# Hybrid decoder trunk on one core: longest query blocks first, and the wait for attention moved into the out-projection

## The chip, the cores and the metric

One core of a Trainium2 chip runs the whole layer in one launch. The metric is device time in microseconds (us) of one execution, lower is better. TensorE (PE) does the matmuls and the transposes, PEld is its weight load, DVE, ACT and POOL do elementwise work, and the queue of SyncE (SP) issues nearly all DMAs.

## The reference, cut to what matters

```python
h = rmsnorm(x, norm_mix_w) * (1 + sc1) + sh1            # 2048 tokens x 1024
hq, hf, hi, hg, sq, sk, sv, iq, ik, iw, cu = split(h @ w_in)
o_a = hgrn2_mixer(hq, hf, hi, hg)                       # linear recurrence, 512 columns
# o_b, 256 columns, one block of 128 queries at a time (16 blocks, j = 0..15):
score = einsum('bqh,bqhs->bqs', iw, relu(q_idx . k_idx)) # 8 indexer heads, keys <= query
sel   = top_k(score, 256)                               # per query
o_b   = softmax(q . k[sel]) @ v[sel]                    # 4 heads of 64
o_c = conv_module(cu)                                   # 256 columns
x = x + g1 * (concat[o_a, o_b, o_c] @ w_out)            # the out-projection
h = rmsnorm(x, norm_mlp_w) * (1 + sc2) + sh2
x = x + g2 * (relu(h @ mlp_w1)**2 @ mlp_w2)             # d_ff 4096
out = rmsnorm(x, final_norm_w)
```

Block j sees (j + 1) x 128 keys, so its indexer, its top-k search and its attention all grow with j.

## The kernel before

**Order of the whole.** Tokens go in four blocks of 512 (b = 0 to 3). First `in_block` projects all four and writes the queries, the keys, the values and the mixers' outputs to DRAM. Then, for each b, comes the out-projection `out_block(b)` and the MLP: `mlp_block` for b = 0 to 2 and `strassen_block` for the last. Matrix products run in three passes of split fp32 (high x high, low x high, high x low); `split` makes the halves, the high one with a copy on ACT (L256), the low one with a subtraction on POOL (L264).

**Background work.** The query blocks j = 0 to 5 are handled during `in_block`, those from `J1` = 6 on beside the MLPs of b = 0, 1 and 2. Each block j is three generators: `index_gen` (scores: PE L752, ACT L754, DVE L759), `topk_gen` (a threshold search on DVE, 8 passes of L861, ending with the bias at L832) and `attn_gen` (PE L909, L931, L943 and L955, DVE L911, ACT L939 and L940, POOL L941), which the search of j appends to its queue when it is done. They sit in the queues "idx", "tk" and "at". A main loop that reaches a `yield` calls `step`, which gives each queue a credit of `rates[q]`; a generator runs until its own yields have used the credit up. Credits are the program's own nominal nanoseconds. The yields are, with n the keys of the block: indexer 8.8 n in all; search 1000 + 7 (1.05 n + 1300) + 2000 + 3.6 n, and 0.6 n after it has handed over (11.55 n + 12100 in all); attention 1.1 n + 4 (1.1 n + 300 c + 300), with c its chunks of 512 keys. A generator that is blocked yields `None` and loses the credit at hand. At most two blocks have their scores alive, and at most two their bias. The tile scheduler then places the instructions on each engine and may let a later one go first where an earlier one isn't ready in its own timeline.

**One MLP block in steps.** `mlp_order` gives 32 `m1` units (first product, L357, PSUM "mm") and 32 `m2` units (second product through `n_unit`, L1169, PSUM "ax", two buffers, evicted by DVE L1313). With group g = 6 it yields "prep" before `m2` of g = 6, and with g = 7 "out" before `m1`. So a block has 52 steps up to "prep", 4 to "out", and 8 after it; `out_block` itself makes 4.

**Where attention is waited for.** "prep" calls `prep_out(b + 1)`, which calls `drain_bg(4 (b + 1) + 3)`: all background queues are pumped with 3000 each, again and again, until the last query block of that token block is done. Then `mix_tiles(b + 1, 0)` loads rows 0 to 3 of the mixed activations (the recurrence). "out" calls `out_block`, which loads x, then `mix_tiles(b, 1)`, rows 4 to 7: rows 4 and 5 are attention, 6 and 7 the convolution. For each of four column blocks q of 256 it runs the first half of the rows (kh = 0) and the second (kh = 1), two token pairs each, in two PSUM buffers "ax" (for b = 0 in "at" and "mm" by turns), 24 matmuls for a pair; DVE L1212 multiplies by the gate, POOL L1216 adds to x.

**Sums for the last MLP.** The queue "ts" runs during `mlp_block(2)`: `tsum_gen` loads 24 units of weight quarters into "tsr", makes four sums each on DVE (L1411, L1412, L1414, L1415) and stores them to `ts_d`. A unit yields 2.0 and the rate is 1.0. At "out" what is left is drained.

Of the kernel before, what the change touches and what calls it, by code (L numbers as in the profile page):

```python
# [8 lines left out]
F32 = mybir.dt.float32  # L9
# [7 lines left out]
OP = mybir.AluOpType  # L17
# [3 lines left out]
P = 128  # L21
# [17 lines left out]
FAST = 979  # L39
# [6 lines left out]
PTB, PM, LB, LB2 = 1, 1, 4, 4  # L46
PREP = 14
R1 = [1126, 1216, 1594]
R2 = [950, 1650, 900]
AXB = 2  # L50
NX = 20
STG = 3
# [25 lines left out]
def trunk(ctx, tc, x, c, ada_w, ada_b, norm_mix_w, norm_mlp_w, w_in, hg_lb_logits,  # L78
# [22 lines left out]
    def nm(s):  # L101
        uid[0] += 1
        return f"{s}_{uid[0]}"

    def dma(o, i):
        return nc.sync.dma_start(o, i)
# [7 lines left out]
    def ps_ax():  # L114
        return px["p"].tile([P, 512], F32, tag="ax", bufs=px["ax"], name=nm("ax"))
# [880 lines left out]

    adone = set()

    def drain_bg(upto=None):
        while any(queues[q] for q in ("idx", "tk", "at")):  # L1000
            if upto is not None and upto in adone:
                break
            for q in ("at", "tk", "idx"):
                pump(q, 3000.0)

    rates = {"fast": FAST, "conv": CR, "ada": 800.0, "ts": 1.0, "idx": R1[0], "tk": R1[1], "at": R1[2]}

    def step():
        for q in ("fast", "conv", "ada", "idx", "tk", "at", "ts"):
# [96 lines left out]

    def out_specs():
        return [([(0, 256, wout[kh * 512:(kh + 1) * 512, q * 256:(q + 1) * 256])], "wo", 4, 256)
                for q in range(4) for kh in range(2)]

    def mlp1_specs(g):
        return [([(0, P, w1[:, (g * 4 + f) * P:(g * 4 + f + 1) * P])], "w1") for f in range(4)]
# [8 lines left out]
    def add_topk(k, js):  # L1121
        for j in js:
            queues["idx"].append(index_gen(k, j))
            queues["tk"].append(topk_gen(k, j))
# [33 lines left out]
            elif what == "m2":  # L1158
                specs += mlp2_specs(g)

    def n_part(ps, tpair, act, w, first, last):
        hh, hl = act
        hi, lo = w
        for t in range(2):
            tok = tpair * 2 + t
            n = 0
            for aa, ww in ((hh, hi), (hl, hi), (hh, lo)):
                for f in range(4):
                    T.matmul(ps[:, t * 256:(t + 1) * 256], aa[f][:, tok * P:(tok + 1) * P],  # L1169
                             ww[:, f, :], start=(first and n == 0 and (last or t == 0)),  # L1170
                             stop=(last and n == 11), skip_group_check=not (first and last))
                    n += 1

    def n_unit(act, consume):
        w = next_w()
        for tpair in range(2):
            ps = ps_ax()
            n_part(ps, tpair, act, w, True, True)
            consume(tpair, ps.rearrange("p (t m) -> p t m", t=2))

    def mix_tiles(b, kh):
        hh, hl = [], []
        for k in range(4):
            hi = mp.tile([P, TB], F32R, tag="hh", bufs=HB, name=nm("mh"))
            lo = mp.tile([P, TB], F32R, tag="hl", bufs=HB, name=nm("ml"))
            r = mp.tile([P, TB], F32, tag="hr", bufs=MR, name=nm("mr"))
            dma(r, mx_d[b][kh * 4 + k])
            split(r, hi, lo)
            hh.append(hi)
            hl.append(lo)  # L1190
        return hh, hl

    def out_block(b, mix0):
        xts = []
        for t in range(4):
            xt = xp.tile([P, D], F32, tag="xt", bufs=4, name=nm("x1"))
            dma(xt, x2d[b * TB + t * P:b * TB + (t + 1) * P, :])
            xts.append(xt)
        mixes = [mix0, mix_tiles(b, 1)]
        for q in range(4):  # L1200
            gq = mp.tile([P, 256], F32, tag="gq", bufs=GQ, name=nm("gq"))
            dma(gq, g_d[2][:, q * 256:(q + 1) * 256].to_broadcast([P, 256]))
            pss = []
            for kh in range(2):
                w = next_w()
                for tp_ in range(2):
                    if kh == 0:
                        pss.append(ps_ax() if b else (ps_at, ps_mm)[q % 2]())
                    n_part(pss[tp_], tp_, mixes[kh], w, kh == 0, kh == 1)
                    if kh == 1:  # L1210
                        tmp = mp.tile([P, 2, 256], F32, tag="hr", bufs=MR, name=nm("ot"))
                        V.tensor_tensor(tmp, pss[tp_].rearrange("p (t m) -> p t m", t=2),  # L1212
                                        gq[:, None, :].to_broadcast([P, 2, 256]), OP.mult)
                        for t in range(2):
                            dst = xts[tp_ * 2 + t][:, q * 256:(q + 1) * 256]
                            G.tensor_tensor(dst, dst, tmp[:, t, :], OP.add)  # L1216
            yield
        for t in range(4):
            xt = xts[t]
            dma(x1_d[b][t], xt)  # L1220
            dump = xp.tile([P, D], BF16, tag="tf", bufs=2, name=nm("xdump"))
            rs = rstd_of(xt, D, dump, "x1")
            V.tensor_scalar(xt, xt, rs, None, op0=OP.mult)
        x1s[b] = xts
# [4 lines left out]
    def mlp_last(acc, act, b):  # L1229
        fw = xp.tile([P, D], F32, tag="xt", bufs=4, name=nm("fw"))  # L1230
        dma(fw, final_norm_w[None, :].to_broadcast([P, D]))
        ss = mp.tile([P, 4, 4], F32, tag="ssq", bufs=1, name="ssq")
        s1 = mp.tile([P, 4], F32, tag="ss1", bufs=1, name="ss1")
        for q in range(4):
            sl = slice(q * 256, (q + 1) * 256)
            gq = mp.tile([P, 256], F32, tag="gq", bufs=GQ, name=nm("gq"))
            dma(gq, g_d[5][:, sl].to_broadcast([P, 256]))
            xq_ = xp.tile([P, 4, 256], F32, tag="xt", bufs=4, name=nm("xq"))
            for t in range(4):
                dma(xq_[:, t], x1_d[b][t][:, sl])  # L1240
            if q == 3:
                V.tensor_tensor(acc[:, :, sl], acc[:, :, sl], gq[:, None, :].to_broadcast([P, 4, 256]), OP.mult)
                V.tensor_tensor(acc[:, :, sl], acc[:, :, sl], xq_, OP.add)

            def consume(tp_, src, q=q, sl=sl, gq=gq, xq_=xq_):
                tt = range(tp_ * 2, tp_ * 2 + 2)
                dst = acc[:, tp_ * 2:tp_ * 2 + 2, sl]
                gv = gq[:, None, :].to_broadcast([P, 2, 256])
                if q == 3:
                    tmp = mp.tile([P, 2, 256], F32, tag="hr", bufs=MR, name=nm("lt"))  # L1250
                    V.tensor_tensor(tmp, src, gv, OP.mult)
                    V.tensor_tensor(dst, dst, tmp, OP.add)
                else:
                    V.tensor_tensor(dst, dst, src, OP.add)  # L1254
                    V.tensor_tensor(dst, dst, gv, OP.mult)
                    V.tensor_tensor(dst, dst, xq_[:, tp_ * 2:tp_ * 2 + 2], OP.add)
                for t in tt:
                    dump = mp.tile([P, 256], BF16, tag="ld", bufs=2, name=nm("ld"))
                    A.activation(dump, acc[:, t, sl], AF.Square, accum_out=ss[:, t, q:q + 1])
                if q == 3:  # L1260
                    rs = s1[:, tp_ * 2:tp_ * 2 + 2]
                    V.tensor_reduce(rs, ss[:, tp_ * 2:tp_ * 2 + 2, :], axis=AX.X, op=OP.add)
                    rpow(rs, rs, 2, 1.0 / D)
                    for t in tt:
                        V.scalar_tensor_tensor(acc[:, t, :], acc[:, t, :], s1[:, t:t + 1], fw,
                                               op0=OP.mult, op1=OP.mult)
                        dma(out2d[b * TB + t * P:b * TB + (t + 1) * P, :], acc[:, t, :])

            n_unit(act, consume)
            if (b, q) == (NB - 2, EQ):  # L1270
                st3["early"]()
            yield

    def mlp_block(b):
# [3 lines left out]
        for what, g, f in mlp_order(b):  # L1278
# [23 lines left out]
            elif g == 7 and b == NB - 2:  # L1302
                yield from mlp_last(acc, hid.pop(g), b)
                return
            else:
                hg_ = hid.pop(g)
                for q in range(4):
                    def consume(tp_, src, q=q):
                        dst = acc[:, tp_ * 2:tp_ * 2 + 2, q * 256:(q + 1) * 256]
                        if g == 0:  # L1310
                            A.copy(dst, src)
                        else:
                            V.tensor_tensor(dst, dst, src, OP.add)  # L1313

                    n_unit(hg_, consume)
                    yield
        fw = xp.tile([P, D], F32, tag="xt", bufs=4, name=nm("fw"))
        dma(fw, final_norm_w[None, :].to_broadcast([P, D]))
# [320 lines left out]
    mixes = {}  # L1639

    def prep_out(b):
        if 4 * b + 3 >= J1:
            drain_bg(4 * b + 3)
        mixes[b] = mix_tiles(b, 0)

    def run_out(b):
# [49 lines left out]
    S3 = ExitStack()  # L1696
    tp2 = S3.enter_context(tc.tile_pool(name="tk2", bufs=1, reuse_waits="tile"))
    k2 = TK(tp2, 2048, SB)
    add_topk(k2, range(J1, 16))
    rates.update({"idx": R2[0], "tk": R2[1], "at": R2[2]})  # L1700
    for b in range(NB):
        if b == NB - 2:
# [33 lines left out]
```

## Time and profile before

| | us |
|---|---|
| median of 3 runs | 3050.99 (3048.38 to 3053.09) |
| profiled execution, its time | 3049.01 |
| its span, first to last instruction | 3047.3 |
| PE busy in the span | 2831.7 |

The span and the profiled execution's own time differ by 1.7 us, which lies around the instructions. The granted clock of PE over the whole span is 0.968 of full speed. A busy PE isn't the same as a PE at full clock: the windows list the granted clock beside the busy time.

### The profile page before, as it was taken

What the parts mean: (1) busy time and instruction counts of PE and PEld (TensorE: products, weight loads), DVE (VectorE), ACT (ScalarE), POOL (GpSimd) and SP (SyncE); (2) the same over time, 40 slices, a digit from 0 to 9 for tenths busy, and PEclk for the clock granted to TensorE, in tenths of its full rate; (3) what the DMA queues carried; (4) which work ended last, traced back from release to release, by engine and by line L of the source; (5) the groups of instructions that cost most, each with busy time, mean ns of one, the idle gap of its engine ahead of it and who ended that gap; (6) DMA issues with size and microseconds to landing.
All of it is one profiled execution on the core that took longest, in us unless ns stands there. A gap on an engine that the chain in (4) does not pass through costs nothing. (4 is left out here: it accounts for less than half of the span.)

```text
span 3047.3 us, 50794 instructions
## 1 busy us (share of the span) xinstructions
PE 2831.7 (93%) x18352; PEld 2549.2 (84%) x18352; DVE 2007.2 (66%) x3673; ACT 1541.7 (51%) x2885; POOL 1796.5 (59%) x1530
## 2 busy tenths in 40 slices
PE   6989989899999999999999999999899997989997
PEld 4878868777887889899988898898788896879997
DVE  7796486977536343757766756577888631487787
ACT  3436354535413234555556555646464543456654
POOL 7565152234305265666777666778676664767775
PEclk9989989999999989999999999999999997999999
DMA  8866756665655343444455444555999943465533
GB/s 269 279 195 237 228 183 222 198 204 179 224 181 165 120 157 100 122 133 138 151 171 193 144 142 136 156 159 177 284 316 298 310 146 107 135 201 180 179 124 114
DMA packets 479416, 560.10 MB, mean 184 GB/s; under 512 B 32615, under 2 KB 371884, under 8 KB 479148
## 3 DMA queue, kind: packets, MB, share of 16 engines
q1 hardware_dynamic: 478992, 556.65, 58.2%
q8 instruction: 145, 2.38, 0.3%
q14 instruction: 123, 1.01, 0.1%
q10 hardware_dynamic: 156, 0.07, 0.0%
HBM read 458.30 MB, written 98.31 MB: 183 GB/s over the span
## 5 line engine op out<-in xcount | busy, mean ns | idle before, releaser
L264 POOL TENSOR_TENSOR wlo<-wraw,whi 128x512 fp32r<-128x512 f32 x514 | 719.5, 1421 | 417.3 <-ACT whi L256 275.0
L256 ACT CAST whi<-wraw 128x1024 fp32r<-128x1024 f32 x257 | 269.7, 1049 | 391.1 <-PE ax L1169 154.5
L759 DVE SCALAR_TENSOR_TENSOR s<-r,iw_s,s 128x512 f32<-128x512 f32 (+3 forms) x266 | 267.8, 1007 | 160.6 <-ACT r L754 159.1
L357 PE MATMUL mm<-ah,wk 128*128 128x512 f32 x1104 | 297.2, 404 | 11.0 <-DVE q L586 3.1
L1169 PE MATMUL ax<-whi,hh 128*128 128x256 f32 x1600 | 276.2, 288 | 22.3 <-DVE acc L1254 8.2
L1169 PE MATMUL ax<-whi,hl 128*128 128x256 f32 x1600 | 274.7, 285 | 2.4 <-POOL hl L264 2.4
L1169 PE MATMUL ax<-wlo,hh 128*128 128x256 f32 x1600 | 272.0, 285 | 0.0
L357 PE MATMUL mm<-ah,whi 128*128 128x512 f32 x936 | 259.2, 403 | 13.6 <-DVE slo L470 3.2
L941 POOL TENSOR_TENSOR pT<-L,pT 128x512 fp32r<-128x512 f32 (+3 forms) x160 | 198.6, 1243 | 116.2 <-ACT pT L940 96.2
L357 PE MATMUL mm<-al,whi 128*128 128x512 f32 x936 | 258.9, 399 | 0.0
L1169 PEld LDWEIGHTS ax<-whi,hh 128*128 128x128 f32 x1600 | 231.4, 191 | 32.7 <-DVE acc L1313 14.6
L357 PEld LDWEIGHTS mm<-ah,wk 128*128 128x128 f32 x1104 | 207.7, 193 | 55.8 <-ACT k L577 3.5
L357 PE MATMUL mm<-ah,wlo 128*128 128x512 f32 x936 | 252.4, 394 | 0.0
L1169 PEld LDWEIGHTS ax<-whi,hl 128*128 128x128 f32 x1600 | 230.5, 191 | 6.2 <-POOL hl L264 3.7
L528 POOL TENSOR_TENSOR cside<-cside,ctap 128x512 f32<-128x512 f32 x112 | 159.1, 1421 | 122.1 <-ACT ctap L527 107.1
L1169 PEld LDWEIGHTS ax<-wlo,hh 128*128 128x128 f32 x1600 | 227.7, 190 | 1.5
L357 PEld LDWEIGHTS mm<-ah,whi 128*128 128x128 f32 x936 | 175.9, 192 | 52.0 <-DVE slo L470 4.0
L754 ACT ACTIVATE r<-ix 128x512 f32<-128x512 f32 (+3 forms) x256 | 141.4, 552 | 145.3 <-PE ix L752 139.0
L357 PEld LDWEIGHTS mm<-al,whi 128*128 128x128 f32 x936 | 176.3, 191 | 35.8
L357 PEld LDWEIGHTS mm<-ah,wlo 128*128 128x128 f32 x936 | 175.2, 189 | 35.8
L861 DVE TENSOR_SCALAR_CACHE_REDUCE cum<-s,ssm 128x384 bf16<-128x384 f32 (+13 forms) x112 | 165.3, 1476 | 2.6 <-POOL s L763 0.4
L1313 DVE TENSOR_TENSOR acc<-acc,ax 128x512 f32<-128x512 f32 x160 | 109.1, 682 | 84.1 <-PE ax L1169 83.9
(551 smaller groups left out, 6881.5 us busy)
## 6 DMA issues: line engine op xcount, KB each, us to landing
wraw<-in_mlp_w_dram SPq DMA_DIRECT2D x192, 512.0 KB, 4.4
wk<-wk_d SPq DMA_DIRECT2D x174, 512.0 KB, 4.9
kc<-sk_d SPq DMA_DIRECT2D x112, 256.0 KB, 3.5
vc<-v_d SPq DMA_DIRECT2D x112, 256.0 KB, 3.6
tsr<-in_mlp_w_dram SPq DMA_DIRECT2D x96, 256.0 KB, 6.3
ts_d<-tsr SPq DMA_DIRECT2D x48, 512.0 KB, 5.9
wr<-in_mlp_w_dram SPq DMA_DIRECT2D x96, 256.0 KB, 3.9
wr<-ts_d SPq DMA_DIRECT2D x72, 256.0 KB, 4.8
```

Of the source, the lines that this page charges most:

```text
L256: A.copy(hi, src)
L264: e.tensor_tensor(lo[:, i:j], src[:, i:j], hi[:, i:j].bitcast(F32), OP.subtract)
L357: T.matmul(ps, ww[:, k, :], aa[k], start=(n == 0 and k0 == 0), stop=(n == len(order) - 1 and k1 == NK))
L528: G.tensor_tensor(side, side, tap, OP.add)
L754: A.activation(r[:, :w], ps[:, :w], AF.Relu, scale=32.0 ** -0.5)
L759: V.scalar_tensor_tensor(s[:, c0:c0 + w], r[:, :w], iw, s[:, c0:c0 + w], op0=OP.mult, op1=OP.add)
L861: V.tensor_scalar(dump, s, t, -AIM - i * STEP, op0=OP.is_ge, op1=OP.add, accum_out=d)
L941: G.tensor_tensor(pT[:, :nt, 1], lv, pT[:, :nt, 0].bitcast(F32), OP.subtract)
L1169: T.matmul(ps[:, t * 256:(t + 1) * 256], aa[f][:, tok * P:(tok + 1) * P], ww[:, f, :], start=(first and n == 0 and (last or t == 0)), stop ...
L1313: V.tensor_tensor(dst, dst, src, OP.add)
```

## The change

The blocks from 6 on are queued in the order 7, 6, 11, 10, 9, 8, 15, 14, 13, 12. `prep_out` no longer drains. `out_block` takes its columns in pairs: first half of the rows for q and q + 1 (a step after each), then the second half for both, convolution rows first. Only ahead of the attention rows of its very first column block does it drain, up to the smallest j of the token block, and load these rows. It makes six steps. Odd columns go to PSUM "mm". `n_unit` can put chosen rows ("late") behind the others of both token pairs. The rates of "idx", "tk" and "at" in the MLPs and of "ts" are new.

```diff
-R2 = [950, 1650, 900]
+R2 = [900, 1950, 940]
...
+    ORDER = [j for b in range(NB) for j in range(4 * b + 3, 4 * b - 1, -1) if j >= J1]
+    LAST = {b: max(4 * b, J1) for b in range(1, NB)}
...
-    rates = {..., "ts": 1.0, ...}
+    rates = {..., "ts": 0.8, ...}
...
-                for q in range(4) for kh in range(2)]
+                for q0 in (0, 2) for kh in range(2) for q in (q0, q0 + 1)]
...
-    def n_part(ps, tpair, act, w, first, last):
+    def n_part(ps, tpair, act, w, first, last, fs=(0, 1, 2, 3)):
...
-            for aa, ww in ((hh, hi), (hl, hi), (hh, lo)):
-                for f in range(4):
+            for aa, ww in ((hh, hi), (hh, lo), (hl, hi)) if len(fs) < 4 else ((hh, hi), (hl, hi), (hh, lo)):
+                for f in fs:
...
+    def n_unit(act, consume, late=()):
         w = next_w()
+        pss = {}
+        for fs in [[f for f in range(4) if f not in late], list(late)]:
+            for tpair in range(2) if fs else ():
+                if tpair not in pss:
+                    pss[tpair] = ps_ax()
+                last = not late or fs[0] in late
+                n_part(pss[tpair], tpair, act, w, fs[0] not in late, last, tuple(fs))
+                if last:
+                    consume(tpair, pss[tpair].rearrange("p (t m) -> p t m", t=2))
...
+        mix1 = mix_tiles(b, 1, (2, 3))
+        for q0 in (0, 2):
...
+            for q in (q0, q0 + 1):
                 w = next_w()
                 for tp_ in range(2):
+                    pss[q, tp_] = ((ps_ax if b else ps_at), ps_mm)[q % 2]()
+                    n_part(pss[q, tp_], tp_, mix0, w, True, False)
+                yield
+            for q in (q0, q0 + 1):
+                w = next_w()
+                gq = gqs[q - q0]
+                for tp_ in range(2):
+                    n_part(pss[q, tp_], tp_, mix1, w, False, False, (2, 3))
+                if q == 0:
+                    if b:
+                        drain_bg(LAST[b])
+                    mix_tiles(b, 1, (0, 1), mix1)
+                for tp_ in range(2):
+                    n_part(pss[q, tp_], tp_, mix1, w, False, True, (0, 1))
                     ... gate, add to x
...
-            n_unit(act, consume)                       # mlp_last
+            n_unit(act, consume, ((3,) if b < NB - 1 else (1, 3)) if q == 0 else ())
...
-                    n_unit(hg_, consume)               # m2 of mlp_block
+                    n_unit(hg_, consume, (3,) if q == 0 and g >= 6 else ())
...
     def prep_out(b):
-        if 4 * b + 3 >= J1:
-            drain_bg(4 * b + 3)
         mixes[b] = mix_tiles(b, 0)
...
-    add_topk(k2, range(J1, 16))
+    add_topk(k2, ORDER)
```

## Rows read from the trace of the kernel before

**Rows 1.** The page: span and engine rows.

```profile
span 3047.3 us, 50794 instructions
...
PE 2831.7 (93%) x18352; PEld 2549.2 (84%) x18352; DVE 2007.2 (66%) x3673; ACT 1541.7 (51%) x2885; POOL 1796.5 (59%) x1530
```

**Rows 2.** Windows: stretch, length, busy PE PEld DVE ACT POOL (instructions), PEclk, DMA share, GB/s.

```profile
1096.00:1130.00 34.00, 26.41 (x145) 22.17 (x144) 19.59 (x29) 15.11 (x36) 16.04 (x19) 0.75 0.50 175
1560.00:2070.00 510.00, 500.51 (x3289) 453.06 (x3288) 337.99 (x624) 294.23 (x541) 361.01 (x306) 1.00 0.51 154
2140.00:2300.00 160.00, 144.51 (x902) 130.05 (x903) 135.48 (x201) 87.54 (x163) 105.77 (x78) 0.95 0.99 302
2300.00:2420.00 120.00, 116.12 (x755) 105.47 (x755) 104.77 (x175) 59.77 (x104) 79.65 (x61) 1.00 0.99 314
2420.00:2530.00 110.00, 109.10 (x736) 100.13 (x736) 31.39 (x60) 54.86 (x97) 73.52 (x62) 1.00 0.53 164
2530.00:2582.00 52.00, 29.25 (x126) 22.68 (x125) 4.55 (x18) 22.15 (x46) 21.20 (x21) 0.64 0.32 99
2582.00:2640.00 58.00, 58.00 (x403) 54.37 (x402) 10.82 (x12) 20.04 (x27) 44.54 (x47) 1.00 0.41 130
2640.00:2720.00 80.00, 64.17 (x461) 59.69 (x460) 66.05 (x72) 47.21 (x101) 53.02 (x41) 0.94 0.61 194
```

**Rows 3.** Waits of PE, 2530 to 2582 us.

```profile
PE ax L1169 <- ACT mh L256: 7.3, 2, 5.3
PE at L955 <- POOL ot L953: 5.9, 3, 3.9
```

**Rows 4.** Lines: PE in 2530 to 2582 us, attention alone.

```profile
L943 PE MATMUL po<-pT,vc 128*128 128x256 f32 x44 | 10.6, 380 | 6.0 <-POOL pT L941 4.6 <-DMA vc<-v_d 1.4
L931 PE MATMUL at<-ident,L 128*128 128x128 f32 x36 | 8.5, 393 | 2.0 <-ACT L L925 2.0
L909 PE MATMUL at<-kc,qs 128*128 128x512 f32 x10 | 4.3, 522 | 0.7 <-ACT L L939 0.7
```

**Rows 5.** Windows of L1169 alone, the same stretch.

```profile
2530.00:2582.00 52.00, 6.74 (x31) 5.64 (x30) 0.64 0.32 99
```

**Rows 6.** Timeline of PE at full clock: pitch of each form.

```profile
2521.28 0.60 PE L931 MATMUL at<-ident,L 128*128 128x128 f32 x4
2521.64 0.61 PE L1169 MATMUL ax<-whi,hl 128*128 128x256 f32 x3
...
2523.16 0.64 PE L943 MATMUL po<-pT,vc 128*128 128x256 f32 x4
2523.63 0.51 PE L1169 MATMUL ax<-whi,ml 128*128 128x256 f32 x3
```

**Rows 7.** Tile bn and line L832: search begins, bias written.

```profile
L845 DVE BATCH_NORM_STATS2 bn<-s x10: 680/685/695, 1168.0 to 2225.6; 128x6 f32<-128x512 f32 x10
...
L832 DVE TENSOR_SCALAR bias<-s x10: 816/1102/1795, 1246.1 to 2454.8; 128x896 bf16<-128x896 f32 x1, 128x1024 bf16<-128x1024 f32 x1, 128x1152 bf16<-128x1152 f32 x1, 128x1280 bf16<-128x1280 f32 x1
```

**Rows 8.** Waits of PE, 2140 to 2420 us.

```profile
PE ax L1169 <- DVE acc L1313: 5.7, 5, 1.8
PE ax L1169 <- DVE sm L827: 5.0, 1, 5.0
...
PE ax L1169 <- POOL hl L264: 1.5, 1, 1.5
```

**Rows 9.** Tile tsr: one of its sums; DMA issues of the page.

```profile
L1415 DVE TENSOR_TENSOR tsr<-tsr x24: 670/693/1761, 2150.3 to 2413.7; 128x512 f32<-128x512 f32 x24
...
tsr<-in_mlp_w_dram SPq DMA_DIRECT2D x96, 256.0 KB, 6.3
ts_d<-tsr SPq DMA_DIRECT2D x48, 512.0 KB, 5.9
```

**Rows 10.** Lines: POOL in 2530 to 2582 us.

```profile
L941 POOL TENSOR_TENSOR pT<-L,pT 128x512 fp32r<-128x512 f32 x9 | 11.4, 1270 | 8.0 <-ACT pT L940 7.0 <-POOL pT L941 0.9
L264 POOL TENSOR_TENSOR ml<-mr,mh 128x512 fp32r<-128x512 f32 x4 | 5.0, 1270 | 6.8 <-ACT mh L256 6.8
```

More of the change, by code (lines that the diff above doesn't have):

```diff
@@ L1004, in drain_bg @@
                 pump(q, 3000.0)
-    rates = {"fast": FAST, "conv": CR, "ada": 800.0, "ts": 1.0, "idx": R1[0], "tk": R1[1], "at": R1[2]}
+    rates = {"fast": FAST, "conv": CR, "ada": 800.0, "ts": 0.8, "idx": R1[0], "tk": R1[1], "at": R1[2]}
     def step():
@@ L1166, in n_part, with mix_tiles @@
             n = 0
-            for aa, ww in ((hh, hi), (hl, hi), (hh, lo)):
-                for f in range(4):
+            for aa, ww in ((hh, hi), (hh, lo), (hl, hi)) if len(fs) < 4 else ((hh, hi), (hl, hi), (hh, lo)):
+                for f in fs:
                     T.matmul(ps[:, t * 256:(t + 1) * 256], aa[f][:, tok * P:(tok + 1) * P],
                              ww[:, f, :], start=(first and n == 0 and (last or t == 0)),
-                             stop=(last and n == 11), skip_group_check=not (first and last))
+                             stop=(last and n == 3 * len(fs) - 1), skip_group_check=not (first and last))
                     n += 1
-    def n_unit(act, consume):
+    def n_unit(act, consume, late=()):
         w = next_w()
[L1176 to L1183, printed above, removed]
+        pss = {}
[7 more added lines that the diff above has]
+                    consume(tpair, pss[tpair].rearrange("p (t m) -> p t m", t=2))
+    def mix_tiles(b, kh, ks=range(4), into=None):
+        hh, hl = into or ([None] * 4, [None] * 4)
+        for k in ks:
             hi = mp.tile([P, TB], F32R, tag="hh", bufs=HB, name=nm("mh"))
@@ L1188, in mix_tiles @@
             split(r, hi, lo)
-            hh.append(hi)
-            hl.append(lo)
+            hh[k], hl[k] = hi, lo
         return hh, hl
@@ L1198, in out_block @@
             xts.append(xt)
[L1199 to L1204, printed above, removed]
+        mix1 = mix_tiles(b, 1, (2, 3))
+        for q0 in (0, 2):
+            gqs, pss = [], {}
+            for q in (q0, q0 + 1):
+                gq = mp.tile([P, 256], F32, tag="gq", bufs=GQ, name=nm("gq"))
+                dma(gq, g_d[2][:, q * 256:(q + 1) * 256].to_broadcast([P, 256]))
+                gqs.append(gq)
+            for q in (q0, q0 + 1):
@@ L1205, in out_block @@
                 w = next_w()
                 for tp_ in range(2):
[L1207 to L1216, printed above, removed]
+                    pss[q, tp_] = ((ps_ax if b else ps_at), ps_mm)[q % 2]()
@@ new lines, in out_block @@
+                    n_part(pss[q, tp_], tp_, mix0, w, True, False)
+                yield
+            for q in (q0, q0 + 1):
+                w = next_w()
[8 more added lines that the diff above has]
+                    n_part(pss[q, tp_], tp_, mix1, w, False, True, (0, 1))
+                    tmp = mp.tile([P, 2, 256], F32, tag="hr", bufs=MR, name=nm("ot"))
+                    V.tensor_tensor(tmp, pss[q, tp_].rearrange("p (t m) -> p t m", t=2),
+                                    gq[:, None, :].to_broadcast([P, 2, 256]), OP.mult)
+                    for t in range(2):
+                        dst = xts[tp_ * 2 + t][:, q * 256:(q + 1) * 256]
+                        G.tensor_tensor(dst, dst, tmp[:, t, :], OP.add)
```

## Prediction

> **What bounds the kernel now.** I read the page first: of a span of 3047.3 us PE is busy in 2831.7 [rows 1]. [...] From 1560 to 2070 us, with background work beside the first two MLPs, PE is busy in 500.5 of 510 us at full clock. From 2420 to 2530 it is busy in 109.1 of 110, and in the out-projection of the last token block (2582 to 2640) in all 58. Between these two lies a hole: from 2530 to 2582 PE is busy in 29.25 of 52 us, at a mean granted clock of 0.64, and DVE, ACT and POOL are mostly idle as well. No engine bounds that stretch; a chain does. The second worst stretch is 2140 to 2420, in which the "ts" sums run: 15.5 and 3.9 us idle, a clock of 0.95 in the first 160 us, DMA share 0.99, and DVE busy in 135 of 160 and 105 of 120 us.
>
> The waits of PE name the chain in the hole: the split of a `mix_tiles` row (L256, 7.3 us), then attention's own link through POOL (5.9 us) [rows 3]. The lines show that nearly all that PE does there is attention: 44 matmuls of L943, 36 transposes of L931, 10 matmuls of L909 [rows 4], with 31 of the out-projection [rows 5]. This is the drain of j = 15: the main line has nothing left beside it but the first column block, which holds both "ax" buffers.
>
> **Why there is a drain.** The credits give it without any engine's time. The ten blocks from 6 to 15 have 128 x (7 + ... + 16) = 14,720 keys, so the search asks for 11.55 x 14,720 + 10 x 12,100 = 291,000 nominal ns, which at 1650 a step is 176 steps. Ahead of it goes the indexer of j = 6 (8.8 x 896 / 950 = 8 steps), behind it the attention of j = 15 (17,260 / 900 = 19). Together 203 steps, where 2 x 68 + 52 = 188 lie before the "prep" of the last token block. The 15 missing steps are some 13,500 of the 17,260 nominal ns of the last attention, to be drained at one go. The trace bears this out: from the first search to the last bias are 1168.0 to 2454.8 us [rows 7], 1287 us for 176 steps or 7.3 us a step, and the last attention ends a hundred microseconds after that bias, in the hole.
>
> **The change part by part.**
>
> *Order, rates, drain (the main term).* At 1950 the search needs 291,000 / 1950 = 149 steps; ahead of it j = 7 (9011 / 900 = 10), behind it j = 12 (15,150 / 940 = 16): 175 steps, and perhaps 12 lost where a generator finds its input missing and forfeits credit, so 175 to 187. The other queues aren't longer: indexer 8.8 x 14,720 / 900 = 144, attention, by the sum of its yields, 131,400 / 940 = 140. The wait now stands after 2 x 70 + 56 + 2 = 198 steps, as out-projections make six steps. Attention should be through 11 to 23 steps, 80 to 170 us, ahead; the drain finds nothing to do. For the first two token blocks the wait was no loss and remains none. What is saved is the hole less the work in it. At full clock a 256-column matmul goes every 0.12 us (four in 0.47), a transpose every 0.09 (four in 0.36) [rows 6]; the 512-column L909 I take at twice 0.12, an estimate. So 44 x 0.12 + 36 x 0.09 + 10 x 0.24 + 31 x 0.12 = 14.6, with five small transposes 15 us. The hole costs 52 - 15 = 37 us. Attention's 11 us of it must now be fitted in earlier, where PE is full; it is counted in the 15. Not all of the 37 comes back: the four splits of rows 4 to 7, 5.0 us of POOL [rows 10], were made in the hole and now fall into the out-projection, where POOL is already busy in 44.5 of 58 us [rows 2]. I take 5 us for that: **-32** (bounds -14, if half the hole returns, and -37).
>
> *The "ts" stage.* At 0.8 a step the 24 units take 60 steps instead of 48, so a fifth less DMA and DVE work a step, and the search is through some 30 steps into that block instead of running beside all of it. The stage loses 19.4 us of idle time and up to 160 x 0.05 = 8 us by the clock [rows 2]; 10.7 us of the waits are for DVE, behind sums and search [rows 8]. In the first half the search runs denser, in the second it is gone. I take a quarter of 27: **-6** (bounds +6, -18).
>
> *Denser background earlier.* Search and attention run 18% and 4% denser through 1130 to 2140, the indexer 5% thinner. DVE is busy there in 338 of 510 us [rows 2]; if all its work grew by 18% it would be 78%, still not the bound. PE idles 9.5 us in these 510; over twice the stretch, and growing by about a fifth: **+4** (bounds 0, +12). The row for a contention here: a sum of 128x512 on DVE takes 0.67 us at least and 1.76 at most [rows 9], and POOL's `pT` 1.27 in the hole, where DVE stands nearly still [rows 10]. [...]
>
> *Rows put late in `n_unit`* (five second-product units, g = 6 and 7). The gain is the wait for the last low half, 1.5 us where it is seen [rows 8], at two places: -3 at most. Against it both "ax" buffers are held to the end of the unit, and the next unit comes six matmuls (0.7 us) after the first is complete, while an eviction is one DVE pass over 512 columns, about the 0.69 us of rows 9: up to 0.5 us each time. **-1** (bounds -3, +3). In `mlp_last` (two places) the first eviction comes 18 matmuls, 2.1 us, later, in a stretch where DVE is busy in 66 of 80 us [rows 2]: **+1** (bounds -2, +4).
>
> *Pairs of columns.* Same matmuls, twice the PSUM, no wait in either order (2582 to 2640 has no idle time): 0. The two added steps in the out-projection of b = 0 bring the recurrence's last head forward; behind it PE is busy in 26.4 of 34 us at clock 0.75 [rows 2]: **-2** (bounds 0, -4).
>
> Sum: -32 - 6 + 4 - 1 + 1 - 2 = -36 from the profiled execution's 3049.0, so **3013**; that execution lies 2 us under the median of the runs.
>
> **Rivals.**
>
> 1. *The hole is only half closed.* The steps count emissions, not engines: if DVE falls behind in the denser stretch, the last attention still trails into the out-projection. For it: DVE at 85% or more in the "ts" stage. Against: 11 steps or more of slack, and two more column halves as cover. -14 instead of -32: 3031.
>
> 2. *The end of "ts" collides with the out-projection.* 56 steps at 0.8 issue 23 of 24 units; the last is drained at "out", and its tiles are those that the x rows need. Load 6.3, four sums 2.8, store 5.9 [rows 9], 15 us and more ahead of the x loads, on the SP queue that also fetches weights. Cover: 2 x 48 + 24 matmuls, 14 us. Price 5 to 15: 3018 to 3028.
>
> 3. *Slower: the denser search starves PE.* One mechanism, from 1130 to 2300 us: PE stands in order, and each eviction or score that waits behind a 2 us search pass on DVE stops it. It decides if the idle time there, about 31 us from 1560 to 2300 with 2070 to 2140 taken like the stage behind it, more than doubles. At +50: 3062. Against it: DVE is no more than two thirds busy up to 2070.
>
> 4. *Nothing happens*: a wait of like size takes the hole's place (the attention rows' store, load and split now behind the drain): 3049. It needs the drain to find work, against the count above.
>
> **How the numbers follow.** Forecast 0.62, its own range 3000 to 3025 from the bounds; rival 1 0.14; rival 2 0.11; rival 3 0.07; rival 4 0.06. The range, 2992 to 3046, reaches down to the sum with most of the "ts" bound and the whole hole, and up through rivals 1 and 2. About 0.2%, 6 us, is what a measurement of this kernel tells from no change. Faster 0.87, same 0.06, slower 0.07.
>
> **What would show it.** Right: PE busy without a hole, at clock 1.00, from the last "prep" to the end of that out-projection; the store of j = 12's attention well before its row loads; the last bias near 2270 to 2340 us instead of 2455; idle time of the "ts" stage below 19 us. Wrong: waits for L256 or for attention in the last out-projection (rival 1 or 4), waits for x or weight loads there (2), or idle time spread over 1130 to 2300 on DVE and POOL (3).

## Result and the profile after

The changed kernel takes 3008.7 us (3008.1 to 3011.4, 4 runs) where the kernel before takes 3052.0 in the same comparison: 0.9853 of the time before, 95% interval 0.9839 to 0.9867, so 41 to 49 us faster. Five more runs in a later group, against nine of the kernel before on the same chip, gave 0.9844 (0.9825 to 0.9863). One run of e12 below took 4375.6 us at a granted clock of 0.577 and is counted in no figure here. Forecast were 3013 us and a range of 2992 to 3046, from a profiled execution of 3049.0; the profiled execution after took 3011.4.

The page after has the same number of matmuls in a span 37.6 us shorter. Busy PE is 22 us less. The same matmuls count longer where the granted clock is lower (in this trace four of 256 columns go every 0.86 us at 0.50, from 2242.17 us, and every 0.48 at 1.00, from 2247.02), and there is less of that now: the granted clock over the span rose from 0.968 to 0.975, and the share that it lacks, times the span, fell from 97 to 75 us, 22 us less as well.

```profile
span 3009.7 us, 50821 instructions
...
PE 2809.9 (93%) x18352; PEld 2539.2 (84%) x18352; DVE 1997.2 (66%) x3673; ACT 1545.7 (51%) x2885; POOL 1787.0 (59%) x1530
```

The windows of the kernel after, in the columns of [rows 2], at the stages that answer to them (the first and the last are shifted, as that work moved):

```profile
1102.00:1136.00 34.00, 23.60 (x130) 19.41 (x130) 17.43 (x24) 18.59 (x40) 18.70 (x23) 0.80 0.66 216
1560.00:2070.00 510.00, 505.34 (x3329) 460.25 (x3328) 339.78 (x631) 304.61 (x556) 367.75 (x313) 1.00 0.52 158
2140.00:2300.00 160.00, 145.24 (x894) 130.09 (x893) 138.52 (x204) 91.09 (x169) 112.40 (x84) 0.95 0.92 290
2300.00:2420.00 120.00, 113.92 (x747) 102.31 (x747) 96.90 (x166) 59.40 (x108) 84.49 (x65) 1.00 1.01 315
2420.00:2530.00 110.00, 110.00 (x753) 101.72 (x751) 25.93 (x66) 59.54 (x112) 72.99 (x66) 1.00 0.61 194
2530.00:2600.00 70.00, 68.77 (x500) 65.08 (x499) 12.96 (x14) 24.26 (x36) 54.20 (x57) 1.00 0.42 134
```

The hole has gone. From 2530 to 2600 us PE is busy in 68.8 of 70 us at clock 1.00, where the stretch from 2530 to 2582 before had 29.25 of 52 at 0.64 [rows 2]. The prediction priced the hole at 37 us and the span is 37.6 us shorter, but that the two agree is chance: the span takes in every other part of the change too. The other stages moved by a few microseconds each, both ways: idle 4.7 us from 1560 to 2070 (9.5 before), 14.8 and 6.1 in the "ts" stage (15.5 and 3.9 before), and behind the first out-projection 10.4 of 34 us (7.6 before).

What is left at the former hole is one wait for the split of an attention row. Waits of PE, 2530 to 2600 us, after:

```profile
PE ax L1172 <- ACT mh L256: 1.1, 1, 1.1
```

It is the remainder of a close finish. The timeline of SP after shows the last block's attention being stored at 2546.97, and the loads of its rows right behind:

```profile
2546.97 0.81 SPq L106 DMA_DIRECT2D mx_d<-ot  x2
2548.55 2.06 SPq L106 DMA_DIRECT2D mr<-mx_d  x2
```

The last search ended at 2385 us, by line L832 after:

```profile
L832 DVE TENSOR_SCALAR bias<-s x10: 679/1245/2237, 1253.2 to 2385.4; 128x1024 bf16<-128x1024 f32 x1, 128x896 bf16<-128x896 f32 x1, 128x1536 bf16<-128x1536 f32 x1, 128x1408 bf16<-128x1408 f32 x1
```

That is 70 us sooner than before [rows 7], though later than the forecast 2270 to 2340; and from that bias to the store lie 162 us.

### The profile page after: what moved, and what is told of

The parts are those of the page before. It is cut to its first block, busy times and chain, and to the rows that moved or that the text cites. A ratio compares the mean times of both kernels' runs of the same rounds, so it can differ in the third digit from the quotient of the medians.

```text
span 3009.7 us, 50821 instructions
## 1 busy us (share of the span) xinstructions
PE 2809.9 (93%) x18352; PEld 2539.2 (84%) x18352; DVE 1997.2 (66%) x3673; ACT 1545.7 (51%) x2885; POOL 1787.0 (59%) x1530
## 5 line engine op out<-in xcount | busy, mean ns | idle before, releaser
L1172 PE MATMUL ax<-wlo,hh 128*128 128x256 f32 x1600 | 280.0, 285 | 0.0
L1334 DVE TENSOR_TENSOR acc<-acc,ax 128x512 f32<-128x512 f32 x160 | 108.9, 682 | 84.9 <-PE ax L1172 84.5
```

## Experiments

All ratios are to the kernel before, on the same chip as the experiment, with their 95% intervals.

**The rates alone (e1).** The kernel before with one line changed:

```diff
-R2 = [950, 1650, 900]
+R2 = [900, 1950, 940]
```

> The kernel before with the three new rates of idx, tk and at alone; drain, order, column order and ts as before. Theory A (the rates decide): by the count of steps attention now ends at step 182 of the 188 before the drain, the drain emits nothing, and most of the hole is gone: 25 to 30 us faster than before, about 3023 us. Theory B (the cover behind which attention ends decides, because the engines run some steps behind the emission): in the changed kernel attention's last rows were only ready at 2553 us, with all of the added cover used up, so without the cover a hole of 12 to 25 us stays: 12 to 20 us faster, about 3035 us.

Measured: 0.9914 (0.9899 to 0.993), 26 us faster. The windows of e1 around the former hole:

```profile
2440.00:2510.00 70.00, 70.00 (x466) 64.18 (x465) 16.34 (x32) 36.17 (x64) 44.93 (x40) 1.00 0.60 190
2510.00:2560.00 50.00, 44.85 (x318) 42.36 (x317) 5.83 (x9) 16.11 (x23) 32.51 (x26) 0.97 0.41 130
2560.00:2600.00 40.00, 40.00 (x320) 39.29 (x319) 5.56 (x9) 11.38 (x15) 28.72 (x32) 1.00 0.38 116
```

and its last store of attention on SP:

```profile
2511.58 0.97 SPq L106 DMA_DIRECT2D mx_d<-ot  x2
```

The hole is closed by the rates alone: 5.2 us idle at clock 0.97 are left from 2510 to 2560, the rest runs full. Attention was stored at 2511.6, some 40 us before PE came to the second half of the rows. Theory A holds, theory B's 12 to 25 us hole isn't there. The new rates have a price, though, beside the first two MLPs. There PE is idle 13.7 us from 1560 to 2070 in e1, where it was 9.5 before [rows 2]:

```profile
1560.00:2070.00 510.00, 496.27 (x3232) 449.34 (x3231) 351.97 (x646) 307.46 (x570) 357.77 (x300) 0.99 0.52 155
```

**The place alone (e2).** The changed kernel with the old rates:

```diff
-R2 = [900, 1950, 940]
+R2 = [950, 1650, 900]
...
-    rates = {..., "ts": 0.8, ...}
+    rates = {..., "ts": 1.0, ...}
```

> The changed kernel with the old rates (idx 950, tk 1650, at 900, ts 1.0): order, place of the drain, pairs, late rows stay. By the count the drain has three rounds of 3000 to emit at step 198, where it had five at step 188. Theory A: the hole stays for the most part: 5 to 15 us faster than before, about 3041 us. Theory B: the cover takes 17 us off the hole at any rate: 17 to 25 us faster, about 3030 us. If both hold, e1 and e2 together give about the 43 us of the whole change.

Measured: 0.999 (0.9978 to 1.0003), no difference that can be told. The windows of e2, and the longest waits of PE from 2550 to 2600:

```profile
2440.00:2550.00 110.00, 108.14 (x739) 100.38 (x738) 28.26 (x58) 55.84 (x100) 74.97 (x66) 0.98 0.49 148
2550.00:2600.00 50.00, 34.92 (x186) 29.40 (x185) 5.66 (x22) 21.25 (x50) 20.17 (x22) 0.69 0.32 99
```

```profile
PE ax L1172 <- ACT mh L256: 5.3, 1, 5.3
PE at L955 <- POOL ot L953: 3.0, 3, 1.0
PE po L943 <- POOL pT L941: 1.7, 5, 0.4
```

With the old rates the drain inside the out-projection finds as much to wait for as the drain ahead of it. The hole is in its new place, 15 us idle at clock 0.69, with the waits of [rows 3] in it. The hole stays, as theory A had it, but A's 5 to 15 us aren't there either. The cover came out worth far less than theory B's 17 us; B falls.

**The "ts" rate (e3).** The changed kernel with

```diff
-    rates = {..., "ts": 0.8, ...}
+    rates = {..., "ts": 1.0, ...}
```

> The changed kernel with ts at 1.0 again. My term for the ts stage was -6 us, a part of which was the lower ts rate: I expect 3 to 5 us slower than the changed kernel, about 3013 us. Rival: the rate only shifts the sums (the changed kernel's ts stage still idles 20.8 us from 2140 to 2420, no less than before), so no difference: 3009 us.

Measured: 0.9866 (0.9847 to 0.9885), which overlaps 0.9853 and 0.9844 of the changed kernel: a difference isn't shown. The chain below settles it for the other order of blocks.

**No late rows (e4).** The changed kernel with both calls of `n_unit` as before:

```diff
-            n_unit(act, consume, ((3,) if b < NB - 1 else (1, 3)) if q == 0 else ())
+            n_unit(act, consume)
...
-                    n_unit(hg_, consume, (3,) if q == 0 and g >= 6 else ())
+                    n_unit(hg_, consume)
```

> The changed kernel with no row put late in n_unit, in mlp_block and mlp_last. My terms were -1 and +1 us: no difference that can be told, 3006 to 3012 us. Rival: the late rows save the waits for the last low half at each of the seven places, 1.5 us each: up to 8 us slower without them, 3017 us.

Measured: 0.9885 (0.9869 to 0.99), 10 us worse than 0.9853, with intervals that don't overlap, though not measured side by side. That speaks against my term of nothing, so the chain below measures it again.

**The changed kernel again (e5).** No edit.

> The changed kernel as it is, on the chip of this group, so that the others can be set against it: 0.9853 of the time before, as measured.

Measured: 0.9844 (0.9825 to 0.9863), 3009.7 us; single runs went from 3007.8 to 3018.4.

**Ascending order (e6).**

```diff
-    ORDER = [j for b in range(NB) for j in range(4 * b + 3, 4 * b - 1, -1) if j >= J1]
-    LAST = {b: max(4 * b, J1) for b in range(1, NB)}
+    ORDER = list(range(J1, 16))
+    LAST = {b: 4 * b + 3 for b in range(1, NB)}
```

> The changed kernel with the blocks from 6 on in ascending order again (the drain then waits for 4 b + 3). By the count of steps attention ends at step 182 instead of 187, so longest first costs five steps of the search's handovers. Theory A (steps): attention ends some 35 us earlier than in the changed kernel, the wait of 1.1 us for its rows goes, and the time is the same within 2 us. Rival (the order is what makes the tail short): the last block is now j = 15 with 2048 keys instead of j = 12 with 1664, its tail is longer, and the time is 5 to 15 us worse.

Measured: 0.9812 (0.9796 to 0.9828), 2999.9 us, 10 us faster than e5 on the same chip; none of its five runs (2998.4 to 3004.9) reaches e5's fastest. The last two stores of attention and the loads of rows on SP in e6, and its windows:

```profile
2365.56 1.21 SPq L106 DMA_DIRECT2D mx_d<-ot  x2
...
2502.56 0.80 SPq L106 DMA_DIRECT2D mx_d<-ot  x2
...
2504.36 1.57 SPq L106 DMA_DIRECT2D mr<-mx_d  x2
```

```profile
2140.00:2300.00 160.00, 150.96 (x953) 134.57 (x952) 143.29 (x211) 94.82 (x174) 122.44 (x88) 1.00 0.99 309
2300.00:2420.00 120.00, 113.69 (x740) 103.76 (x740) 92.55 (x146) 56.25 (x97) 80.65 (x62) 0.99 1.01 318
...
2530.00:2600.00 70.00, 70.00 (x502) 66.15 (x501) 12.84 (x16) 28.63 (x42) 56.89 (x58) 1.00 0.41 133
```

Attention ends at 2502.6 us, 44 us sooner than in the changed kernel, where the count of steps had some 35, and PE waits for no row. The rival falls: longest first made nothing shorter. But the 1.1 us at the rows don't explain 10 us. Most of them lie in the first part of the "ts" stage: PE is idle 9.0 us from 2140 to 2300 at clock 1.00, where the changed kernel is idle 14.8 at 0.95.

**No cover (e7).** Columns one by one, attention rows first:

```diff
-                for q0 in (0, 2) for kh in range(2) for q in (q0, q0 + 1)]
+                for q in range(4) for kh in range(2)]
...
-        for q0 in (0, 2):
+        for q0 in range(4):                      # "for q in (q0, q0 + 1)" becomes "for q in (q0,)"
...
-                    n_part(pss[q, tp_], tp_, mix1, w, False, False, (2, 3))
+                    n_part(pss[q, tp_], tp_, mix1, w, False, False, (0, 1))   # behind the drain
...
-                    n_part(pss[q, tp_], tp_, mix1, w, False, True, (0, 1))
+                    n_part(pss[q, tp_], tp_, mix1, w, False, True, (2, 3))
```

> The changed kernel without the cover ahead of the attention rows: columns one by one instead of in pairs, and the attention rows first in the second half, the convolution rows behind them; rates, order, number of steps and drain inside the out-projection stay. That takes away 48 + 24 + 24 matmuls of 0.12 us, 11 us, that now run between the last unit before the out-projection and the attention rows. As the prediction had it (attention is through 80 to 170 us ahead) nothing changes: within 3 us of the changed kernel. Rival (in the trace after, the attention rows came 1.1 us late with all of this cover used): a wait of 12 us, and some more by the clock: 10 to 18 us slower than the changed kernel.

Measured: 0.9854 (0.9838 to 0.9869), 3014.9 us against 3009.7; the intervals overlap, so the time decides nothing here. The trace does. The longest wait of PE from 2530 to 2600 us in e7 is for the attention rows, and the store on SP comes when it came in the changed kernel:

```profile
PE ax L1172 <- ACT mh L256: 5.3, 1, 5.3
```

```profile
2547.01 0.82 SPq L106 DMA_DIRECT2D mx_d<-ot  x2
```

The wait is 5.3 us instead of 1.1. So the cover hides about 4 us in the changed kernel, not none, as the prediction's head start would have it, and not the 11 of the rival: part of the later work is fitted in ahead of the wait anyway.

**Higher rates (e8).**

```diff
-R2 = [900, 1950, 940]
+R2 = [1000, 2200, 1100]
```

> The changed kernel with still higher rates (1000, 2200, 1100). By the count attention ends at step 165 instead of 187. If the rates only have to close the hole, nothing is left to win: within 3 us of the changed kernel. Rival (denser background starves PE from 1130 to 2300 us, my third rival): 5 to 15 us slower.

Measured: 0.9851 (0.9828 to 0.9873), the same as the changed kernel. The windows of e8 show both sides:

```profile
1560.00:2070.00 510.00, 496.08 (x3234) 449.92 (x3233) 340.74 (x636) 307.10 (x565) 360.32 (x304) 0.99 0.50 156
...
2530.00:2600.00 70.00, 70.00 (x543) 68.11 (x542) 12.18 (x16) 21.11 (x28) 51.37 (x53) 1.00 0.44 141
```

The out-projection runs without a pause (70 of 70), and from 1560 to 2070 PE is idle 13.9 us where the changed kernel is idle 4.7. The waits that grew most are for attention's `pT` from POOL (4.8 us, none in the changed kernel) and for evictions on DVE (4.4 us instead of 1.4). A denser background does starve PE, by single microseconds, at a fifth of the price of rival 3 and only in part by its mechanism, the wait for DVE.

**A chain on one chip (e9 to e12).** From the rates alone to e6, one part after the other: e9 is e1 again; e10 is e6 with "ts" at 1.0 and the late rows taken out as in e4; e11 puts "ts" at 0.8; e12 puts the late rows back and is e6 again.

> The kernel of e1 again (new rates of idx, tk and at alone), as the first link of a chain on one chip: 0.9914 of the time before, about 26 us faster.

> Second link: e1 and the whole new out-projection (drain inside it, columns in pairs, attention rows last, six steps), ascending order, ts at 1.0, no late rows. If the pairs and the moved wait carry what e1 lacks: 15 to 25 us faster than e9. By my prediction's terms (pairs 0, wait moved past a drain that emits nothing, 5 us of splits and waits behind the hole): 0 to 7 us faster than e9.

> Third link: e10 with ts at 0.8. By e3 (0.9866 against 0.9849 for the changed kernel) 2 to 6 us faster than e10; by the idle time of the ts stage, which the changed kernel did not lower, no difference.

> Fourth link: e11 with the late rows, which is the kernel of e6 again: 0.9812 of the time before. By my terms the late rows are worth nothing (within 3 us of e11); by e4 (0.9885 against 0.9849) they are worth 8 to 12 us.

Measured, in this order:

| | ratio | interval | step |
|---|---|---|---|
| e9, rates | 0.9908 | 0.9891 to 0.9925 | 28 us faster than before |
| e10, and the new out-projection | 0.9893 | 0.9875 to 0.9911 | 5 us, not told from none |
| e11, and "ts" at 0.8 | 0.9888 | 0.9869 to 0.9906 | 2 us, not told from none |
| e12, and the late rows | 0.9829 | 0.9812 to 0.9845 | 18 us, intervals apart |

Between e10 and e11 the traces list the same instructions in the same sequence on PE, DVE, ACT and POOL and the same DMAs on SP: with ascending order this change of the "ts" rate changes nothing. That the four "xt" buffers hold the stage back, and not the credits, would explain it, but no run changed their number. The two are one program measured twice.

The late rows are the surprise. The windows of the first 130 us behind the third out-projection (behind the start of its last gate product), in e11 and e12, both in ascending order, without and with late rows:

```profile
2085.40:2215.40 130.00, 117.52 (x680) 103.32 (x678) 109.29 (x159) 79.24 (x144) 100.71 (x88) 0.93 0.66 198
```

```profile
2063.00:2193.00 130.00, 126.42 (x801) 112.27 (x800) 105.46 (x175) 91.63 (x174) 112.57 (x93) 1.00 0.79 243
```

and in e4 and the changed kernel, both longest first, again without and with late rows:

```profile
2068.30:2198.30 130.00, 117.83 (x712) 103.48 (x712) 109.59 (x157) 83.11 (x154) 105.68 (x86) 0.97 0.74 227
```

```profile
2060.10:2190.10 130.00, 119.27 (x727) 105.18 (x728) 112.99 (x161) 83.18 (x154) 104.85 (x85) 0.97 0.74 226
```

The longest waits of PE from 2070 to 2240 us, e11:

```profile
PE ax L1173 <- DVE acc L1335: 3.6, 1, 3.6
PE at L909 <- DVE mx L911: 3.3, 1, 3.3
PE at L873 <- DVE ssm L862: 2.3, 1, 2.3
PE ax L1173 <- POOL hl L264: 2.2, 1, 2.2
```

and e12:

```profile
PE po L943 <- POOL pT L941: 1.9, 2, 1.3
PE ax L1173 <- POOL hl L264: 0.9, 2, 0.8
```

In these 130 us PE is idle 12.5 us at clock 0.93 in e11 and 3.6 us at 1.00 in e12. With longest first it is idle 12.2 us without late rows and 10.7 with them, at 0.97 both times: there the late rows bring little. In e11 the wait of 3.6 us for an eviction, at 2148 us, is among the units of g = 7, the first of which has the late rows; the waits for a score (L911), a search pass (L873) and a low half (2.2 us, at 2199) come 30 to 70 us behind it, in code that the edit doesn't touch.

## Why the prediction was right, and where it wasn't

**The main term held, in mechanism.** The hole was one chain, the count of credits said why, and the rates alone close it (e1 and e9, 26 and 28 us faster); without the rates the moved wait wins nothing (e2). PE's busy share and clock at the place are as forecast. The 26 and 28 us are not the main term alone, though: they hold the price of the denser background too. The traces tell the two apart. The table gives the time that PE lost in the profiled executions: its idle time, and the share that the granted clock lacks times the length, from one out-projection's last gate product to another's (idle time at a granted clock below 1.00 counts in both).

| us lost | before | e1, e9 | changed: result, e5 | e4 | e10, e11 | e6, e12 |
|---|---|---|---|---|---|---|
| order; late rows | asc.; no | asc.; no | longest first; yes | longest first; no | asc.; no | asc.; yes |
| first to third | 28 | 41, 44 | 29, 23 | 29 | 32, 33 | 30, 30 |
| third to last | 77 | 29, 32 | 35, 38 | 32 | 40, 36 | 19, 21 |
| last to the end | 51 | 52, 52 | 50, 52 | 51 | 52, 53 | 49, 51 |

The rates win 45 to 48 us where the hole was, beside the third MLP, and lose 13 to 17 beside the first two. What the rest of the change adds to the rates is won beside the first two MLPs, where nothing was forecast to be won, and not beside the third.

**The head start was mis-sized.** The step that failed is "attention should be through 11 to 23 steps, 80 to 170 us, ahead". By the count the last attention is emitted 11 steps ahead, but it was stored at 2547.0 us and PE stood waiting for its rows at 2552.6: some 6 us instead of 80. The wait on PE's timeline:

```profile
2553.71 0.38 PE L1172 MATMUL ax<-whi,mh 128*128 128x256 f32 x1 [1.06 <-ACT mh L256]
```

The prediction turned steps of emission into engine time, and the engines run behind the emission. The pace was right: the attention of j = 12 is emitted behind that of j = 13, the one ahead of it in its queue, which was stored at 2427.04:

```profile
2427.04 1.80 SPq L106 DMA_DIRECT2D mx_d<-ot  x2
```

From there to its own store are 120 us for 16 steps, 7.5 us a step. In e6 it is 137 us for 18 steps, much the same. What the count left out is the lag. The last bias came at 2385 us, 45 us and more behind the forecast, and the attention of j = 13 was stored 42 us behind that bias. By the credits its 15,856 nominal ns (n = 1792, c = 4) take 17 steps and the search beside it 16, so the two should have ended about one step apart. So the drain that "finds nothing to do" was right, and the slack it stands on was about nothing: what hid the remainder was the cover (e7: 4 us), which the prediction had put at 0. Of the four signs of being right that the prediction named, the one that came is PE without a hole, but for the wait of 1.1 us. The bias was late, the store came 1.6 us before its row loads and not well before, and the "ts" stage idles 20.8 us.

**Order was not priced.** With the handovers of this order attention ends five steps later than ascending. With late rows it costs 10 us (e6 against e5). Without them it costs nothing that can be told: e4 in this order has 0.9885, e11 in ascending order 0.9888, though on different chips, and attention ends about as much later (last store at 2556.3 us against 2505.3). So the late end of attention is not what costs. Beside the third MLP, at these rates, only ascending order and late rows together bring the time lost down, to 19 and 21 us; either alone leaves it at 35 to 40, neither (e4) at 32. The higher rates of e8 reach 20 too, but lose 42 beside the first two MLPs. Why order and late rows work only together was not tested.

**The "ts" term was wrong.** -6 was forecast; idle time there is 20.8 us after and 19.4 before. The rate does nothing by itself (e10 and e11). The longest wait there comes from one engine's order. The three longest waits of PE from 2140 to 2420, after:

```profile
PE ax L1172 <- DVE acc L1334: 10.4, 4, 7.6
PE at L931 <- ACT L L925: 3.7, 1, 3.7
PE po L943 <- POOL pT L941: 3.2, 5, 1.5
```

and the longest of them on the timeline, PE first, then DVE, then the last that POOL does up to 2246 us, with the window of the 10 us from 2236.2 behind it:

```profile
2233.25 0.28 PE L943 MATMUL po<-pT,vc 128*128 128x256 f32 x1
2241.15 1.22 PE L1172 MATMUL ax<-whi,hh 128*128 128x256 f32 x4 [7.62 <-DVE acc L1334]
2242.17 1.05 PE L1172 MATMUL ax<-whi,hl 128*128 128x256 f32 x4
2243.03 1.05 PE L1172 MATMUL ax<-wlo,hh 128*128 128x256 f32 x4
...
2247.02 0.64 PE L1172 MATMUL ax<-whi,hh 128*128 128x256 f32 x4
2247.50 0.64 PE L1172 MATMUL ax<-whi,hl 128*128 128x256 f32 x4
```

```profile
2233.76 1.25 DVE L1433 TENSOR_TENSOR tsr<-tsr,tsr 128x512 f32<-128x512 f32 x1
2234.94 1.22 DVE L829 TENSOR_TENSOR top<-top,sm 128x8 f32<-128x8 f32 x1
...
2236.21 1.70 DVE L1435 TENSOR_TENSOR tsr<-tsr,tsr 128x512 f32<-128x512 f32 x1
...
2237.90 2.00 DVE L830 MATCH_REPLACE8 s<-top,s 128x1792 f32<-128x1792 f32 x1
2239.83 0.68 DVE L1436 TENSOR_TENSOR tsr<-tsr 128x512 f32<-128x512 f32 x1
2240.42 0.68 DVE L1334 TENSOR_TENSOR acc<-acc,ax 128x512 f32<-128x512 f32 x1
```

```profile
2234.42 2.94 POOL L264 TENSOR_TENSOR wlo<-wraw,whi 128x512 fp32r<-128x512 f32 x2
```

```profile
2236.20:2246.20 10.00, 5.05 (x23) 5.05 (x24) 9.25 (x17) 0.37 (x1) 1.29 (x2) 0.50 0.69 218
```

PE stops at 2233.5 for an "ax" buffer, and the eviction L1334 stands in DVE's queue behind three sums (1.25, 1.70 and 0.68 us) and the end of a search, MATCH_REPLACE8 with 2.0 us above all; it starts at 2240.42. Behind the pause four matmuls take 1.02 us from start to start, the next four 0.86, at a granted clock of 0.50 (2236.2 to 2246.2 us); at 1.00, from 2247.02, four take 0.48. This is the mechanism of my rival 3, in one place. DVE's sum takes 1.70 us at 2236.21, beside POOL, and 0.68 at 2239.83, when POOL is idle. Over the whole trace of the changed kernel, 34 of the 96 sums overlap no TENSOR_TENSOR of POOL, and they take 0.67 to 0.69 us; all 28 that take more than 1.5 us overlap one. No run here took POOL away, so that POOL's work is what makes them longer is not shown.

**Late rows were mis-sized most.** My -1, and +1 for `mlp_last`, weighed only the units themselves: 1.5 us saved and 0.5 lost at each place in the one, a later eviction in the other. Measured are 18 us with ascending order (e12 against e11), and some 10 with longest first (e4). With ascending order the trace accounts for it: behind the first out-projection PE loses 123 and 121 us in e10 and e11 and 98 and 102 in e6 and e12, and most of the difference lies beside the third MLP. With longest first it doesn't: there e4 loses 112 us, the changed kernel 114 and 113, and e4's profiled execution came to the end of the first out-projection 3 to 7 us later, by code that is the same. Where e4's 10 us come from stays open. How much is the edit's own doing, by a smooth hand-over at g = 7, and how much is that the scheduler laid out everything behind the first late row anew, stays open: no run keeps that layout and removes the late rows.

**The rest.** Denser background cost nothing in the changed kernel (from 1560 to 2070 idle 4.7 us instead of 9.5, where +4 was forecast). With the rates alone it cost 13 and 17 us by the table (e1 and e9, first to third), above the bound of 12. The pairs of columns were measured only together with the moved wait (e10), and the two aren't told from 0, as forecast. The two steps in the first out-projection won nothing: 10.4 us idle at clock 0.80 behind it, 7.6 at 0.75 before.

So the total came out 7 us better than forecast, and that it came so near is luck: errors offset each other. On the chain's numbers it is -28 for the rates, about -5 for the out-projection, 0 for "ts", -18 for the late rows, +10 for the order. The last two are not terms of their own: taken the other way round, by e4, the order costs nothing and the late rows bring 10.

**A faster version.** e6, the changed kernel with ascending order, beats both: 0.9812 (0.9796 to 0.9828) and, as e12, 0.9829 (0.9812 to 0.9845), about 3002 us where the kernel before takes 3058.

## What to carry to other kernels

When a hand-made schedule drains a background queue, count the queue's credits against the steps ahead of the drain before looking at any engine: the shortfall says whether the rate or the place is at fault, and here only the rate was. Then don't read the head start off the same count; measure how far the engines run behind the emission, at the last result that is stored. And price an edit of a static schedule by a run of that edit alone, with and without the others: what it shifts behind itself can outweigh what it does where it stands, and here late rows and order had no price of their own.

## What the runs showed of the hardware that was not expected

One program's time on one chip isn't better known than to some microseconds: e10 and e11, the same instructions in the same sequence, gave 3019.8 to 3029.4 and 3017.8 to 3030.4 us. The last gate product of the first out-projection, with the same code up to it, began between 1100.7 and 1110.9 us in the profiled executions of the kernels with the new `out_block` (e7 aside), and in two executions of the changed kernel at 1102.7 and 1106.8.

With one pause of 7.6 us, in the changed kernel, PE lost more than the pause: in the records the granted clock was 0.50 for 10 us around it (2236.2 to 2246.2 us), and behind it four 256-column matmuls took 1.02 and then 0.86 us, where at 1.00 they took 0.48.
